# Broadcast rows fetched by DMA, gate columns joined to the key/value strip, and the next group's first products moved ahead of routing, in a one-core decoder layer

## The chip, the cores and the metric

The kernel runs on one core of a Trainium2 chip. The metric is the device time of one execution in microseconds; lower is better. A core has a matrix engine (PE), a vector engine (DVE), a scalar engine (ACT), a general one (POOL, which here issues the gathers and scatters), and SP, which issues the plain transfers in the order in which they stand in its queue. Each engine works through its own instructions in one fixed order and waits for others by semaphores.

## The reference, cut to what matters

For 1024 tokens of 1024 channels:

```python
h = rmsnorm(x, norm1_gain)
(aq, ak, av, mq, mk, mv, mi, mf, mo, gate_a, gate_m) = split_columns(h @ w_in)
att = sliding_window_attention(rope(norm(aq)), rope(norm(ak)), av, sinks)   # 16 query heads, 2 key heads, window 128
i_pre, f_pre = 15 * tanh((mi + i_bias) / 15), 15 * tanh((mf + f_bias) / 15) # 8 + 8 gate columns
hm = mlstm_chunkwise(mq, mk, mv, i_pre, f_pre)                              # 8 heads, a state carried over the tokens
hm = rmsnorm(hm, per head) * sigmoid(mo)
mixed = sigmoid(gate_a) * (att @ w_branch_attn) + sigmoid(gate_m) * (hm @ w_branch_mlstm)
x = x + mixed @ w_out
# experts: 8 heads, each the 16 best of 128 x 128 pairs of sub-keys
q = rmsnorm(x, norm2_gain) @ w_query
s = q . sub_keys;  idx, gate = softmax of the 16 best sums of two scores
x = x + sum over the chosen of gate * gelu(xb . down[idx]) * up[idx]
```

## The kernel before

The 1024 tokens are 8 blocks of 128, taken in 4 groups of two (`GROUPS`). The program has a front, four passes of `front(blocks, fill, hT, following)`, and then `dense()`, in which PE runs all 16,384 experts for blocks 1 to 5. Blocks 0, 6 and 7 (`SPARSE`) get their experts by gathers instead.

One pass of `front` does, in the order of the code: products for the attention's queries (AQ) and for its keys and values (KV); the small products of 16 gate columns with `wif` (L367 to L370); norm and rope of queries and keys; the gates chain, which ends in 8-row tiles `rr` and `wi`; attention (`scores`, `attend`, L429 to L493); mLSTM queries and keys (MQ, MK, into the tile `mqk`); mLSTM values (MV); the decay tile `WT`, made by spreading each row of `rr` over 128 partitions with a product against the identity (L509), adding a triangle with another (L510), and an exponential on ACT; the products of keys and queries (L519); the products that spread `wi` (L528); output gate (MO); the mLSTM output and state, here called the h-stage (L538 to L598); the mixing gates GA, WA, GM, WB (L601 to L620); `normed(following)`, the first norm of the next group; the output products WO (L628); the second norm (L633); and routing, that is the transposes into `xbT`, the router queries WQ (L644) and their scores (L657), which go to memory.

A product with weights takes them as strips `w` of 512 KB through four buffers, in the order of SP's queue. For most products a strip is split in two: ACT casts a high part `whi` (L231), DVE subtracts it for a low part `wlo` (L232), and three matrix products are added (L248 to L250). WA, WB, WO and WQ are not split (L246). The 50 split strips of a group are AQ 8, KV 2, MQ 4, MK 4, MV 8, MO 8, GA and GM 16. The text calls the low part of split strip number n w*n*, counted from 1 over all groups: w101 is the first strip of AQ in the third group, w119 the first of MV there.

`later(blocks)` emits the top-16 selection `topk` of a routed group behind everything of lesser priority (`LATER`): DVE does it in the gaps of the next group. From it come the indices `idx` of block 0, the cells of blocks 1 and 2 (L735), and for blocks 3 to 5 the small products of `spread` (L740 to L767), which `fill` puts one by one beside the products of GA to WQ. POOL gathers 128 rows for block 0 (L773), each consumed on DVE (L787) from three buffers, paced by the products of the front; and it scatters the gates of blocks 1 and 2, 128 instructions each (L804), between the gathers as `BESIDE` says: those of block 1 from gather 24 to 62 on. A scatter that begins a head waits for the 16 of the head before.

A scheduler places the instructions of each engine in one order from priorities and dependences, so a changed program changes that order. PSUM holds three product tiles (`pj`).

Of the kernel before, what the change touches and what calls it, by code (L numbers as in the profile page):

```python
# [12 lines left out]
F32 = mybir.dt.float32  # L13
# [48 lines left out]
def layout(inputs):  # L62
# [3 lines left out]
            np.asarray(inputs["w_out"])[0], np.asarray(inputs["peer_w_query"])[0],  # L66
            w[:, 1024:1280]]
# [4 lines left out]
    a["wif"] = w[:, 3328:3344].reshape(NC, P, 16).transpose(1, 0, 2)  # L72
# [24 lines left out]
def build(nc, tc, a, out, dbg=None):  # L97
# [32 lines left out]
    raw0 = t4([P, 2, P], "raw0")  # L130
    SY.dma_start(raw0[:, 0], a["ident"])
    SY.dma_start(raw0[:, 1], a["tri"])
    identr = cp.tile([P, P], F32R, name="identr")
    trir = st.tile([P, P], F32R, name="trir")
    A.copy(identr, raw0[:, 0])
    A.copy(trir, raw0[:, 1])
# [8 lines left out]
    wifr = t4([P, NC, 16], "wifr")  # L145
    SY.dma_start(wifr, a["wif"])
    wif = [st.tile([P, NC, 16], F32R, name=n) for n in ("wifh", "wifl")]
    A.copy(wif[0], wifr)
    V.tensor_tensor(wif[1], wifr, wif[0].bitcast(F32), ALU.subtract)
    ifb = bcast("ifb", 16, st)  # L150
    band = const("band", [P, 256], pool=st)
    nsinks = bcast("sinks", 16, st)
# [52 lines left out]
    flat = {b: t.rearrange("n i e t -> (n i e t)") for b, t in cells.items()}  # L205
    none = st.tile([P, P * P // ZP], F32, name="none")
# [14 lines left out]
    def wpart(i, q, split):  # L221
        t = wp.tile([P, 4, 256], F32, name="w", bufs=WB)
        SY.dma_start(t, a["wmain"][i, :, 4 * q:4 * q + 4, :])
        for z in [next(clear, None)]:
            if z is not None:
                SY.dma_start(z, none)
        if not split:
            return t, None
        hi = wp.tile([P, 4, 256], F32R, name="whi", bufs=3)
        lo = wp.tile([P, 4, 256], F32R, name="wlo", bufs=3)  # L230
# [27 lines left out]
    def token_major(i, act, nb, n=2, before=nothing):  # L258

        pss = [ppj.tile([P, 512], F32, name="pj") for _ in range(nb)]  # L260
        for u in range(n):
            for q in range(2):
                w = wpart(i + u, q, act[1] is not None)
                for b in range(nb):
                    before()
                    accumulate(pss[b][:, 256 * u:256 * u + 256], pick(act, slice(b * P, (b + 1) * P)),
                               pick(w, slice(0, 256), 4 * q), range(4 * q, 4 * q + 4))
        return [ps[:, :256 * n] for ps in pss]
# [52 lines left out]
    def front(blocks, fill, hT, following):  # L321
# [5 lines left out]
        ms = sp.tile([P, nb, 18], F32, name="qkms")  # L327
        for s in range(3):
            nh = 8 if s < 2 else 2
            pss = token_major(2 * (S_AQ + s) if s < 2 else 2 * S_KV, hT, nb, 2 if s < 2 else 1)  # L330
            for i, b in enumerate(blocks):
# [39 lines left out]
        gt = sp.tile([P, nb, 2, 8], F32, name="gt", bufs=1)  # L371
# [4 lines left out]
        V.tensor_tensor(gf, ps[:, 0:16 * nb].rearrange("p (b k) -> p b k", k=16),  # L376
                        ifb[:, None, :].to_broadcast([P, nb, 16]), ALU.add)
# [38 lines left out]
        A.activation(R[64:72, :tn], m, AF.Exp, scale=-1.0)  # L416
        gc = fp.tile([P, TMAX // P, 72], F32, name="gc")
# [78 lines left out]
        mqk = fp.tile([P, 2, 4, TMAX], F32, name="mqk")  # L496
        mqT, mkT = mqk[:, 0], mqk[:, 1]
        for j, ps in enumerate(feature_major(2 * S_MQ, hT, tn, 4)):
            A.copy(mqT[:, j, :tn], ps)
        for j, ps in enumerate(feature_major(2 * S_MK, hT, tn, 4)):  # L500
            A.activation(mkT[:, j, :tn], ps, AF.Copy, scale=0.125)
# [466 lines left out]
```

## Time and profile before

| what | us |
| --- | --- |
| median of 3 runs | 3464.04 (3463.8 to 3468.68) |
| the profiled execution | 3461.28 |
| its span in the profile | 3459.5 |
| PE busy in the span | 3309.9 (96%) |
| front, up to the first dense product at about 1650 | 1650 |
| dense phase | 1809.5 |

The profile is one execution. Busy time is the time in which an engine has an instruction; the granted clock of PE is given as a share of full speed. A wait is put down to what came last. In the front the four passes overlap at their ends, so a stage's stretch is read from the instructions of its lines.

### The profile page before, as it was taken

To read this page: it belongs to the slowest core of one execution; us is meant where nothing else is said; L and a number is where in the kernel's file an instruction comes from. 1 tells how busy PE (TensorE), PEld (TensorE's weight loads), DVE (VectorE), ACT (ScalarE), POOL (GpSimd) and SP (SyncE) were. 2 spreads that over 40 slices of the span, in tenths; PEclk is the share of its full clock that TensorE was granted. 3 is DMA by queue.
4 is the path that set the end of the run, shared out by engine and by line. 5 is a ranking of instruction groups with operands and counts; after the bars stand their busy time and mean duration, and the time that the engine had idled before them with its cause. 6 is when DMAs were issued, how large, how long until landed. Compare 5 with 4: busy or idle time off the path is not lost.

```text
span 3459.5 us, 54381 instructions
## 1 busy us (share of the span) xinstructions
PE 3309.9 (96%) x20061; PEld 2980.2 (86%) x20061; DVE 2655.4 (77%) x6101; ACT 1289.8 (37%) x2535; POOL 1414.7 (41%) x1028
## 2 busy tenths in 40 slices
PE   7999999987999999997899999999999999999999
PEld 7898988877888888886888889999898989999998
DVE  5342489527889498995999888888888889889885
ACT  6652475225654475545331222222222222222221
POOL 0000001578766475600016545454545545445542
PEclk9899999998999998999999999999999999999999
DMA  7554536786679965877549889888888888888984
GB/s 247 181 169 153 179 117 210 227 233 157 168 208 230 255 182 169 209 213 218 190 149 334 312 309 330 299 322 293 313 298 319 295 308 311 294 311 311 324 286 157
DMA packets 385531, 846.77 MB, mean 245 GB/s; under 512 B 163568, under 2 KB 185840, under 8 KB 385264
## 3 DMA queue, kind: packets, MB, share of 16 engines
q1 hardware_dynamic: 237808, 440.44, 38.7%
q0 software_dynamic: 147456, 402.85, 36.1%
q8 instruction: 158, 2.59, 0.3%
q14 instruction: 109, 0.89, 0.1%
HBM read 780.11 MB, written 63.05 MB: 244 GB/s over the span
## 4 chain that ended last, share of the span: by engine, by line
PE 55%; DVE 11%; DMA 5%; issue 3%; POOL 2%; ACT 1%; DVEq 0%; POOLq 0%; SPq 0%; ACTq 0%
PE ph L860 20%; PE po L883 7%; PE po L887 7%; PE po L886 7%; PE pj L246 4%; PE pj L248 2%; PE pj L250 2%; PE pj L249 2%; PE at L763 2%; DVE g L787 1%; DMA w<-wmain 1%; POOL g L773 1%; DMA g<-up,idx 1%; DMA rawu<-up 1%; DVE oi L755 1%
## 5 line engine op out<-in xcount | busy, mean ns | idle before, releaser
L773 POOL DMA_INDIRECT g<-down,idx x384 | 480.6, 1252 | 1118.9 <-DVE sc L674 506.4
L773 POOL DMA_INDIRECT g<-up,idx x384 | 491.1, 1279 | 755.3 <-DVE acc L821 396.6
L787 DVE CUSTOM_DVE_ANT_0 g<-g,xb 128x1024 f32<-128x1024 f32 x384 | 462.0, 1218 | 124.7 <-DMA g<-down,idx 124.5
L821 DVE SCALAR_TENSOR_TENSOR acc<-g,coef,acc 128x1024 f32<-128x1024 f32 x384 | 491.7, 1280 | 42.4 <-DMA g<-up,idx 31.7
L860 PE MATMUL ph<-xbh,hd 128*128 128x320 f32 x2048 | 470.0, 311 | 35.5 <-ACT hd L848 26.0
L883 PE MATMUL po<-hu,ah 128*128 128x512 f32 x1280 | 499.9, 391 | 1.6 <-ACT ah L872 1.5
L887 PE MATMUL po<-hu,al 128*128 128x512 f32 x1280 | 499.0, 390 | 1.8 <-DVE al L873 1.6
L886 PE MATMUL po<-lu,ah 128*128 128x512 f32 x1280 | 499.2, 390 | 0.0
L804 POOL DMA_INDIRECT cells<-dgate,cell x256 | 442.8, 1730 | 115.0 <-issue 76.5
L860 PE MATMUL ph<-xbh,ld 128*128 128x320 f32 x2048 | 469.8, 311 | 3.3 <-DVE ld L849 3.1
L860 PE MATMUL ph<-xbl,hd 128*128 128x320 f32 x2048 | 469.4, 311 | 0.0
L848 ACT CAST hu<-rawu 128x1024 fp32r<-128x1024 f32 x128 | 131.5, 1052 | 754.1 <-PE po L887 556.4
L860 PEld LDWEIGHTS ph<-xbh,hd 128*128 128x128 f32 x2048 | 345.9, 189 | 39.4 <-ACT hd L848 26.4
L232 DVE TENSOR_TENSOR wlo<-w,whi 128x1024 fp32r<-128x1024 f32 x200 | 243.5, 1219 | 167.3 <-ACT whi L231 165.6
L860 PEld LDWEIGHTS ph<-xbh,ld 128*128 128x128 f32 x2048 | 344.6, 189 | 5.1 <-DVE ld L849 5.1
L860 PEld LDWEIGHTS ph<-xbl,hd 128*128 128x128 f32 x2048 | 345.2, 189 | 0.0
L231 ACT CAST whi<-w 128x1024 fp32r<-128x1024 f32 x200 | 209.2, 1047 | 265.6 <-DMA w<-wmain 105.6
L889 DVE TENSOR_TENSOR y<-po,y 128x512 f32<-128x512 f32 x320 | 218.3, 686 | 90.0 <-PE po L887 89.8
L887 PEld LDWEIGHTS po<-hu,al 128*128 128x128 f32 x1280 | 240.7, 188 | 53.8 <-DVE al L873 3.3
L883 PEld LDWEIGHTS po<-hu,ah 128*128 128x128 f32 x1280 | 240.5, 188 | 53.2 <-ACT ah L872 2.4
L886 PEld LDWEIGHTS po<-lu,ah 128*128 128x128 f32 x1280 | 240.7, 188 | 48.6
L249 PE MATMUL pj<-wlo,hT 128*128 128x256 f32 x832 | 246.3, 297 | 8.4 <-DVE wlo L232 8.4
(276 smaller groups left out, 6579.9 us busy)
## 6 DMA issues: line engine op xcount, KB each, us to landing
w<-wmain SPq DMA_DIRECT2D x328, 512.0 KB, 4.8
rawd<-downT SPq DMA_DIRECT2D x128, 512.0 KB, 7.1
rawu<-up SPq DMA_DIRECT2D x128, 512.0 KB, 5.6
gate_d<-stage SPq DMA_DIRECT2D x24, 1024.0 KB, 6.9
g<-gate_d SPq DMA_DIRECT2D x32, 768.0 KB, 12.0
cells<-none SPq DMA_DIRECT2D x128, 128.0 KB, 4.2
ga<-cells SPq DMA_DIRECT2D x64, 256.0 KB, 8.1
x<-x SPq DMA_DIRECT2D x16, 512.0 KB, 6.8
```

Of the source, the lines that this page charges most:

```text
L231: A.copy(hi, t)
L232: V.tensor_tensor(lo, t, hi.bitcast(F32), ALU.subtract)
L249: T.matmul(ps, lh(c), rl(c), start=False, stop=False)
L773: ins = G.indirect_dma_start(out=t, out_offset=None, in_=a[table], in_offset=bass.IndirectOffsetOnAxis(ap=idx[:, s:s + 1], axis=0))
L787: ins = V.tensor_tensor_reduce(out=t, in0=t, in1=xb, scale=1.0, scalar=0.0, op0=ALU.mult, op1=ALU.add, accum_out=act[:, s:s + 1])
L804: ins = G.indirect_dma_start(out=views[s], out_offset=bass.IndirectOffsetOnAxis(ap=cell[:, c:c + 1], axis=0), in_=vals[:, c:c + 1], in_off ...
L821: ins = V.scalar_tensor_tensor(acc, t, g, acc, ALU.mult, ALU.add)
L860: ins = T.matmul(ps[:, u, 0:W], w[:, c, :], x[:, c, u * W:u * W + W], start=first, stop=last)
L883: first = T.matmul(o, ah[:, tok], uh[:, cols], start=(e == 0), stop=False)
L886: T.matmul(o, ah[:, tok], ul[:, cols], start=False, stop=False)
L887: ins = T.matmul(o, al[:, tok], uh[:, cols], start=False, stop=(e == EG - 1))
L889: V.tensor_tensor(y[:, k, cols], o, y[:, k, cols], ALU.add)
```

## The change

Four edits. The gate columns are no longer products of their own: they are 16 more columns of the KV strips (272 wide). `WT` is no longer filled by PE: `rr` is written to memory (`rr_d`, 8 KB) and read back by a transfer that repeats each row over 128 partitions (1 MB); DVE adds the triangle; the exponential is done in place. `wi` goes the same way through `wi_d` into `wib`, and one DVE multiplication of 128 x 1024 takes the place of four. `front` is a generator that yields twice: once after AQ, KV, MQ and MK, once after the second norm's rows. The loop runs the first part of group n+1 there, then the routing of group n, then the rest of group n+1. So MQ and MK no longer stand behind the attention, and `later` of a group starts after the next group's first products. Lastly the tiles move: the sigmoids of the mixing gates no longer have four buffers `gs`, but lie in `gsa`, which shares its place with `mqk`; `sc` shares with `sm`; `oj` has two buffers.

```diff
--- before.py
+++ after.py
@@ layout, build: inputs @@
-            np.asarray(inputs["w_out"])[0], np.asarray(inputs["peer_w_query"])[0],
-            w[:, 1024:1280]]
+            np.asarray(inputs["w_out"])[0], np.asarray(inputs["peer_w_query"])[0]]
...
-    a["wif"] = w[:, 3328:3344].reshape(NC, P, 16).transpose(1, 0, 2)
+    a["wkv"] = np.concatenate([w[:, 1024:1280], w[:, 3328:3344]], axis=1).reshape(NC, P, 272).transpose(1, 0, 2)
...
+    tri = const("tri", [P, P], pool=st)
...
+    rr_d, wi_d = [dp.tile([8, TMAX], F32, name=n) for n in ("rr_d", "wi_d")]
@@ wpart, token_major @@
-        t = wp.tile([P, 4, 256], F32, name="w", bufs=WB)
-        SY.dma_start(t, a["wmain"][i, :, 4 * q:4 * q + 4, :])
+        n = 272 if i == 2 * S_KV else 256
+        t = wp.tile([P, 4, n], F32, name="w", bufs=WB)
+        SY.dma_start(t, a["wkv"][:, 4 * q:4 * q + 4, :] if n > 256 else a["wmain"][i, :, 4 * q:4 * q + 4, :])
...
@@ front @@
+        gt = sp.tile([P, nb, 2, 8], F32, name="gt", bufs=1)
...
+                    V.tensor_tensor(gt[:, i].rearrange("p k h -> p (k h)"), ps[:, 256:272], ifb, ALU.add)
+        mqk = fp.tile([P, 2, 4, TMAX], F32, name="mqk")
+        mqT, mkT = mqk[:, 0], mqk[:, 1]
+        for j, ps in enumerate(feature_major(2 * S_MQ, hT, tn, 4)):
+            A.copy(mqT[:, j, :tn], ps)
+        for j, ps in enumerate(feature_major(2 * S_MK, hT, tn, 4)):
+            A.activation(mkT[:, j, :tn], ps, AF.Copy, scale=0.125)
+        yield
+
...
-        ps = ppj.tile([P, 512], F32, name="pj")
-        for i in range(nb):
-            accumulate(ps[:, 16 * i:16 * i + 16], pick(hT, slice(i * P, (i + 1) * P)), pick(wif, slice(0, 16)),
-                       range(NC))
...
+        WT = fp.tile([P, 8, TMAX], F32, name="WT", tag="mixT")
+        SY.dma_start(rr_d, rr)
+        SY.dma_start(WT, rr_d[None].to_broadcast([P, 8, tn]))
+        wib = fp.tile([P, 4, TMAX], F32, name="wib")
+        SY.dma_start(wi_d, wi)
+        for e in range(2):
+            SY.dma_start(wib[64 * e:64 * e + 64], wi_d[None, e::2].to_broadcast([64, 4, tn]))
+        V.tensor_tensor(WT.rearrange("p h (b t) -> p (h b) t", t=P), WT.rearrange("p h (b t) -> p (h b) t", t=P),
+                        tri[:, None, :].to_broadcast([P, 8 * nb, P]), ALU.add)
...
-        WT = fp.tile([P, 8, TMAX], F32, name="WT", tag="mixT")
         for h in range(8):
-            ps = ppj.tile([P, 512], F32, name="pj")
-            T.matmul(ps[:, :tn], ident[0:8, h:h + 1].to_broadcast([8, P]), rr, start=True, stop=False)
-            T.matmul(ps[:, :tn], identr, trir[:, None, :].to_broadcast([P, nb, P]), start=False, stop=True)
             for i in range(nb):
-                A.activation(WT[:, h, i * P:(i + 1) * P], ps[:, i * P:(i + 1) * P], AF.Exp, bias=gc[:, i, h:h + 1])
+                w = WT[:, h, i * P:(i + 1) * P]
+                A.activation(w, w, AF.Exp, bias=gc[:, i, h:h + 1])
...
-        for j in range(4):
-            ps = ppj.tile([P, 512], F32, name="pj")
-            for e in range(2):
-                T.matmul(ps[64 * e:64 * e + 64, :tn], ident[0:8, 2 * j + e:2 * j + e + 1].to_broadcast([8, 64]), wi,
-                         start=True, stop=True)
-            V.tensor_tensor(qsT[:, j, :tn], ps[:, :tn], mqT[:, j, :tn], ALU.mult)
-            V.tensor_copy(dec[:, j, 0:nb], ps[:, P - 1:tn:P])
+        V.tensor_copy(dec, wib[:, :, P - 1::P])
+        V.tensor_tensor(qsT, mqT, wib, ALU.mult)
...
-        def gates(i):
-            gs = []
-            for ps in feature_major(i, hT, tn, 4, fill):
-                g = fp.tile([P, TMAX], F32, name="gs", bufs=4)[:, :tn]
-                A.activation(g, ps, AF.Sigmoid)
-                gs.append(g)
-            return gs
+        gsa = fp.tile([P, 2, 4, TMAX], F32, name="gsa", tag="mqk")
+
+        def gates(i, s):
+            for k, ps in enumerate(feature_major(i, hT, tn, 4, fill)):
+                A.activation(gsa[:, s, k, :tn], ps, AF.Sigmoid)
+            return [gsa[:, s, k, :tn] for k in range(4)]
...
+        xbs = norm_rows(xs)
+        for x2, b in zip(xs, blocks):
+            SY.dma_start(x2_d[b], x2)
+        yield nextT
+
         xbT = fp.tile([P, NC, TMAX], F32, name="xbT", tag="mixT")
-        xbs = norm_rows(xs)
...
-                sc = t4([P, 8, P], "sc")
+                sc = fp.tile([P, 8, P], F32, name="sc", tag="sm", bufs=2)
...
-                    oj = ks.tile([P, 2, P], F32, name="oj", bufs=3)
+                    oj = ks.tile([P, 2, P], F32, name="oj", bufs=2)
@@ the loop over the groups @@
-        hT = front(g, fill, hT, GROUPS[n + 1] if n + 1 < len(GROUPS) else None)
-        for _ in spreads:
-            pass
+        part = front(g, fill, hT, GROUPS[n + 1] if n + 1 < len(GROUPS) else None)
+        next(part)
+        if behind:
+            for _ in behind[0]:
+                pass
+            for _ in chain.from_iterable(behind[1]):
+                pass
+            queue.append(chain.from_iterable(later(GROUPS[n - 1])))
+        hT = next(part)
+        behind = part, queue
```

The first place is on PE, between the output products of group 0 (`pj<-w,mixT`) and the next work. Before, the second norm's transposes (`tp<-identr,scr x16`) and the router queries (`pj<-xbT,w`) come next, and then the scores and the first split products of group 1:

```order
L246 MATMUL pj<-w,mixT 128x256 x57
L286 MATMUL tp<-identr,scr 128x128 x16
L246 MATMUL pj<-xbT,w 128x256 x64
L657 MATMUL at<-w,qpT 128x128 x20
L248 MATMUL pj<-whi,hT 128x256
L249 MATMUL pj<-wlo,hT 128x256
L250 MATMUL pj<-whi,hTlow 128x256
```

In the change, the split products of group 1 follow at once, 432 instructions up to the end of MK:

```order
L281 MATMUL tp<-identr,scr 128x128 x8
L240 MATMUL pj<-w,mixT 128x256 x57
L242 MATMUL pj<-whi,hT 128x256
L243 MATMUL pj<-wlo,hT 128x256
L244 MATMUL pj<-whi,hTlow 128x256
```

The norm's transposes and the routing stand behind them, and between the scores come the transposes of the new queries:

```order
L243 MATMUL pj<-hTlow,whi 128x256
L244 MATMUL pj<-hT,wlo 128x256
L281 MATMUL tp<-identr,scr 128x128 x16
L240 MATMUL pj<-xbT,w 128x256 x64
L652 MATMUL at<-w,qpT 128x128 x20
L281 MATMUL tp<-identr,qk 128x128 x4
L652 MATMUL at<-w,qpT 128x128 x8
L281 MATMUL tp<-identr,qk 128x128 x4
```

The AQ, KV, MQ and MK products of the next group moved ahead of the routing.

The second place is on PE behind the MO products of group 1, where the h-stage (`vaug`, `C,mqk`, `kw`, `sg`) meets the mixing gates (`pj<-hT,whi` is GA, `pj<-attT,w` is WA). Before:

```order
L248 MATMUL pj<-hT,whi 128x256
L249 MATMUL pj<-hTlow,whi 128x256
L589 MATMUL at<-vaug,kw 64x129 x4
L250 MATMUL pj<-hT,wlo 128x256
L246 MATMUL pj<-attT,w 128x256 x3
L560 MATMUL at<-vaug,WT 128x129
L562 MATMUL at<-C,mqk 128x129
L560 MATMUL at<-vaug,WT 128x129
L562 MATMUL at<-C,mqk 128x129
L246 MATMUL pj<-attT,w 128x256 x4
L286 MATMUL tp<-identr,sg 128x128
L544 MATMUL tp<-identr,mqk 128x128 x4
```

In the change, after 72 of the 96 GA products of this half:

```order
L242 MATMUL pj<-hT,whi 128x256
L243 MATMUL pj<-hTlow,whi 128x256
L244 MATMUL pj<-hT,wlo 128x256
L281 MATMUL tp<-identr,sg 128x128
L553 MATMUL at<-vaug,WT 128x129
L555 MATMUL at<-C,mqk 128x129
L553 MATMUL at<-vaug,WT 128x129
L555 MATMUL at<-C,mqk 128x129
L582 MATMUL at<-vaug,kw 64x129 x4
L281 MATMUL tp<-identr,sg 128x128 x3
L582 MATMUL at<-vaug,kw 64x129 x4
L553 MATMUL at<-vaug,WT 128x129
```

Here the h-stage now runs as one piece of 30 rows without a product between; the last 24 GA products and all of WA stand behind it.

The third place is on DVE, where the gathered rows of block 0 (`g,act<-g,xb`) stand among the low parts of the strips. Before, the last of 13 such rows that all stand between w100 and w101, and what follows:

```order
L787 ISA g,act<-g,xb 128x1024
L787 ISA act 128x1
L787 ISA g,act<-g,xb 128x1024
L787 ISA act 128x1
L232 TENSOR_TENSOR wlo<-w,whi 128x1024 x3
L787 ISA g,act<-g,xb 128x1024
L787 ISA act 128x1
L232 TENSOR_TENSOR wlo<-w,whi 128x1024
L787 ISA g,act<-g,xb 128x1024
L787 ISA act 128x1
L232 TENSOR_TENSOR wlo<-w,whi 128x1024 x2
L787 ISA g,act<-g,xb 128x1024
```

In the change, in the middle of the same group's AQ and KV strips:

```order
L781 ISA g,act<-g,xb 128x1024
L781 ISA act 128x1
L226 TENSOR_TENSOR wlo<-w,whi 128x1024
L331 TENSOR_REDUCE qkms<-sq 128x8
L781 ISA g,act<-g,xb 128x1024
L781 ISA act 128x1
L226 TENSOR_TENSOR wlo<-w,whi 128x1024
L331 TENSOR_REDUCE qkms<-sq 128x8
L226 TENSOR_TENSOR wlo<-w,whi 128x1024
L781 ISA g,act<-g,xb 128x1024
L781 ISA act 128x1
L226 TENSOR_TENSOR wlo<-w,whi 128x1088 x2
```

By count, gathers 24 to 36 stood ahead of w101 before; now 24 to 30 do, and gathers 31 to 40 stand one or two strips apart between w102 and w117, gathers 41 to 47 ahead of w119. The scatters start on POOL after gather 29 instead of 24.

## Rows read from the trace of the kernel before

**Rows 1.** The page: busy time of the engines, and the chain that ended last.
```profile
PE 3309.9 (96%) x20061; PEld 2980.2 (86%) x20061; DVE 2655.4 (77%) x6101; ACT 1289.8 (37%) x2535; POOL 1414.7 (41%) x1028
PE 55%; DVE 11%; DMA 5%; issue 3%; POOL 2%; ACT 1%; DVEq 0%; POOLq 0%; SPq 0%; ACTq 0%
```

**Rows 2.** Stretches up to and from 1650 us: length, busy time by engine, clock, DMA.
```profile
0.00:1650.00 1650.00, 1522.83 (x10077) 1351.25 (x10077) 1104.99 (x3836) 844.57 (x1988) 598.02 (x388) 0.93 0.68 197
1650.00:3459.50 1809.50, 1787.04 (x9984) 1628.92 (x9984) 1550.43 (x2267) 445.25 (x548) 816.68 (x640) 0.99 0.81 289
```

**Rows 3.** What PE waited for: us in total, times, longest.
```profile
PE tp L286 <- ACT scr L308: 48.3, 5, 22.1
...
PE tp L286 <- DVE qk L357: 13.1, 2, 11.3
...
PE at L657 <- ACT sc L660: 5.5, 4, 2.1
```

**Rows 4.** Instruction groups by form on PE, 0 to 1660 us.
```profile
L509 PE MATMUL pj<-rows,identr 8*128 8x256 f32 x64 | 30.8, 571 | 0.0
...
L519 PE MATMUL at<-mqk 64*128 64x128 f32 x128 | 20.4, 429 | 0.0
L250 PE MATMUL pj<-wifh,hTlow 128*128 128x16 f32 x64 | 18.6, 290 | 0.0
...
L528 PE MATMUL pj<-rows,identr 8*64 8x256 f32 x64 | 15.8, 642 | 0.0
```

**Rows 5.** Stretches inside groups: length, PE, PEld, DVE, ACT, POOL, clock, DMA share, GB/s.
```profile
55.00:62.00 7.00, 7.00 (x57) 7.00 (x56) 0.95 (x5) 4.74 (x9) 0.00 (x0) 0.86 0.88 294
62.00:139.00 77.00, 76.14 (x618) 67.62 (x617) 43.40 (x150) 61.11 (x172) 0.00 (x0) 0.97 0.80 248
139.00:160.00 21.00, 21.00 (x77) 12.17 (x77) 5.27 (x11) 6.32 (x18) 0.00 (x0) 0.57 0.15 54
186.00:226.00 40.00, 39.69 (x268) 34.41 (x267) 20.92 (x81) 30.68 (x80) 0.00 (x0) 1.00 0.30 95
...
948.00:997.00 49.00, 47.26 (x276) 38.34 (x274) 41.81 (x193) 29.93 (x79) 27.51 (x18) 0.93 0.62 166
...
1231.00:1318.00 87.00, 84.29 (x697) 73.93 (x697) 84.09 (x337) 68.39 (x186) 58.89 (x36) 0.96 0.60 157
1318.00:1338.00 20.00, 20.00 (x81) 12.06 (x79) 11.74 (x37) 6.53 (x20) 4.96 (x3) 0.62 0.36 109
```

**Rows 6.** Timeline of PE within the MO products of group 2.
```profile
944.10 0.28 PE L250 MATMUL pj<-whi,hTlow 128*128 128x256 f32 x1
944.22 0.28 PE L248 MATMUL pj<-whi,hT 128*128 128x256 f32 x1
```

**Rows 7.** The instructions of L562, 925 to 1000 us: median ns, first and last start.
```profile
L562 PE MATMUL at<-C,mqk x32: 272/374/501, 948.5 to 988.6; 64*128 64x129 f32 x32
```

**Rows 8.** The page: two DMA issues, the weight strips' remainder on DVE.
```profile
L232 DVE TENSOR_TENSOR wlo<-w,whi 128x1024 fp32r<-128x1024 f32 x200 | 243.5, 1219 | 167.3 <-ACT whi L231 165.6
...
gate_d<-stage SPq DMA_DIRECT2D x24, 1024.0 KB, 6.9
...
cells<-none SPq DMA_DIRECT2D x128, 128.0 KB, 4.2
```

**Rows 9.** What DVE waited for, 640 to 840 us.
```profile
DVE g L787 <- DMA g<-down,idx: 86.8, 17, 10.0
```

**Rows 10.** The scatters on POOL from the first on, to the 128th and 78th.
```profile
645.40:977.00 331.60, 215.62 (x128) 0.90 0.71 185
...
645.40:838.00 192.60, 127.39 (x78) 0.88 0.76 200
```

**Rows 11.** Stretches around the scatters and of group 3, columns as in rows 5.
```profile
645.00:751.00 106.00, 89.44 (x472) 78.98 (x472) 32.79 (x68) 24.15 (x58) 82.84 (x58) 0.94 0.79 203
...
751.00:833.00 82.00, 59.80 (x412) 57.41 (x409) 45.06 (x104) 31.10 (x52) 66.03 (x42) 0.80 0.72 192
...
1195.00:1418.00 223.00, 216.55 (x1547) 189.90 (x1545) 192.61 (x696) 132.28 (x325) 141.06 (x83) 0.90 0.66 186
```

More of the change, by code (lines that the diff above doesn't have):

```diff
@@ L128, in bcast @@
         return const(name, [P, n], a[name].to_broadcast([P, n]), pool=pool)
-    raw0 = t4([P, 2, P], "raw0")
-    SY.dma_start(raw0[:, 0], a["ident"])
-    SY.dma_start(raw0[:, 1], a["tri"])
+    raw0 = t4([P, P], "raw0")
+    SY.dma_start(raw0, a["ident"])
     identr = cp.tile([P, P], F32R, name="identr")
-    trir = st.tile([P, P], F32R, name="trir")
-    A.copy(identr, raw0[:, 0])
-    A.copy(trir, raw0[:, 1])
+    A.copy(identr, raw0)
     ident = identr.bitcast(F32)
@@ L144, in build @@
     qkg = bcast("qkg", 128, st)
[L145 to L149, printed above, removed]
     ifb = bcast("ifb", 16, st)
     band = const("band", [P, 256], pool=st)
+    tri = const("tri", [P, P], pool=st)
     nsinks = bcast("sinks", 16, st)
@@ L228, in wpart @@
             return t, None
-        hi = wp.tile([P, 4, 256], F32R, name="whi", bufs=3)
-        lo = wp.tile([P, 4, 256], F32R, name="wlo", bufs=3)
+        hi = wp.tile([P, 4, n], F32R, name="whi", bufs=3)
+        lo = wp.tile([P, 4, n], F32R, name="wlo", bufs=3)
         A.copy(hi, t)
@@ L260, in token_major @@
         pss = [ppj.tile([P, 512], F32, name="pj") for _ in range(nb)]
+        width = 272 if i == 2 * S_KV else 256
         for u in range(n):
@@ L265, in token_major @@
                     before()
-                    accumulate(pss[b][:, 256 * u:256 * u + 256], pick(act, slice(b * P, (b + 1) * P)),
-                               pick(w, slice(0, 256), 4 * q), range(4 * q, 4 * q + 4))
-        return [ps[:, :256 * n] for ps in pss]
+                    accumulate(pss[b][:, 256 * u:256 * u + width], pick(act, slice(b * P, (b + 1) * P)),
+                               pick(w, slice(0, width), 4 * q), range(4 * q, 4 * q + 4))
+        return [ps[:, :256 * (n - 1) + width] for ps in pss]
     def feature_major(i, act, tn, n, before=nothing):
@@ L365, in front @@
         probe("qT", qT, b0)
-        ps = ppj.tile([P, 512], F32, name="pj")
-        for i in range(nb):
-            accumulate(ps[:, 16 * i:16 * i + 16], pick(hT, slice(i * P, (i + 1) * P)), pick(wif, slice(0, 16)),
-                       range(NC))
-        gt = sp.tile([P, nb, 2, 8], F32, name="gt", bufs=1)
         g1 = sp.tile([P, nb, 8], F32, name="g1", tag="g1", bufs=1)
@@ L375, in front @@
         gf = gt.rearrange("p b k h -> p b (k h)")
-        V.tensor_tensor(gf, ps[:, 0:16 * nb].rearrange("p (b k) -> p b k", k=16),
-                        ifb[:, None, :].to_broadcast([P, nb, 16]), ALU.add)
         A.activation(gf, gf, AF.Tanh, scale=1.0 / 15.0)
@@ L494, in front @@
         probe("attT", attT, b0)
[L496 to L501, printed above, removed]
         for s in range(2):
@@ L601, in front @@
         mixT = fp.tile([P, 8, TMAX], F32, name="mixT")
-        def gates(i):
-            gs = []
-            for ps in feature_major(i, hT, tn, 4, fill):
-                g = fp.tile([P, TMAX], F32, name="gs", bufs=4)[:, :tn]
-                A.activation(g, ps, AF.Sigmoid)
-                gs.append(g)
-            return gs
+        gsa = fp.tile([P, 2, 4, TMAX], F32, name="gsa", tag="mqk")
[3 more added lines that the diff above has]
+            return [gsa[:, s, k, :tn] for k in range(4)]
         for s in range(2):
-            gs = gates(2 * (S_GA + s))
+            gs = gates(2 * (S_GA + s), s)
             for k, ps in enumerate(feature_major(2 * (S_WA + s), (attT, None), tn, 4, fill)):
@@ L615, in front @@
         for s in range(2):
-            gs = gates(2 * (S_GM + s))
+            gs = gates(2 * (S_GM + s), s)
             for k, ps in enumerate(feature_major(2 * (S_WB + s), (hmT, None), tn, 4, fill)):
@@ L620, in front @@
                 V.tensor_tensor(mx_, mx_, gs[k], ALU.add)
-        hT = normed(following) if following else None
+        nextT = normed(following) if following else None
         xs = []
@@ L636, in front @@
             transposed(xbT[:, :, i * P:(i + 1) * P], xb, gains[:, 2])
-            SY.dma_start(x2_d[b], x2)
             if b in SPARSE:
@@ L661, in front @@
                 SY.dma_start(sc_d[b, q], sc)
-        return hT
     def topk(b):
@@ L921, in build, with fill @@
     hT = normed(GROUPS[0])
+    behind = None
     for n, g in enumerate(GROUPS):
-        spreads = chain.from_iterable(later(GROUPS[n - 1])) if n else iter(())
+        queue = []
         due = [0.0]
-        def fill():
+        def fill(queue=queue, due=due):
             due[0] += QUADS
             while due[0] >= 1.0:
-                next(spreads, None)
+                for q in queue:
+                    next(q, None)
                 due[0] -= 1.0
-        hT = front(g, fill, hT, GROUPS[n + 1] if n + 1 < len(GROUPS) else None)
-        for _ in spreads:
-            pass
+        part = front(g, fill, hT, GROUPS[n + 1] if n + 1 < len(GROUPS) else None)
[8 more added lines that the diff above has]
+        behind = part, queue
+    for _ in behind[0]:
+        pass
+    for _ in chain.from_iterable(behind[1]):
+        pass
     later(GROUPS[-1])
```

## The prediction

> **What bounds the kernel now.** I read the page's busy times first: PE works in 96% of the span and holds over half of the chain that ended last [rows 1]. Cutting the span where the dense phase begins shows two regimes. From 1650 us on PE is busy for 1787 of 1809.5 us; nothing of the change touches that phase, so it stays. In the front PE is busy for 1523 of 1650 us and idle for 127 [rows 2]. So nearly all that can be won lies in PE's own work in the front and in those 127 us. The list of PE's waits says what they are: 48.3 us for the normed rows `scr` before transposes (22.1 of it at the very start, which stays), 13.1 for the roped `qk`, 5.5 for the router scores' evacuation [rows 3]. DVE is the second engine: in the front it works 1105 us, and in the stretch of group 3 from 1195 us it is busy 192.6 of 223 us [rows 2, 11]. There is one stretch in which neither bounds. From 645 to 833 us PE is busy only 149 of 188 us [rows 11], DVE waits 86.8 us for gathered rows in 17 pieces [rows 9], and POOL is in the middle of 128 scatters that last 331.6 us [rows 10]. There the chain of scatter, gather, DVE, low part of a strip, product sets the pace.
>
> **Removed: the gate columns.** Their 192 small products stand in four stretches of 7 us, of which the first is shown [rows 5]; each takes 0.29 us, though only 16 wide [rows 4]. In the strip they are 16 more columns on 48 products per group; at 0.12 us per 256 columns [rows 6] that is 0.4 us. Sum over four groups: -26 us.
>
> **Removed: the row products.** Between attention and MO stand four stretches of 21, 24, 19 and 20 us (first and last shown, [rows 5]), in which PE is busy throughout at a granted clock of 0.57 and 0.62 in those shown. What stays of them is L519, 20.4 us in all [rows 4]. That is 84 - 20.4 = 64 us less, 16 in a group. The busy time of the removed kinds agrees: 30.8 and 15.8 us for L509 and L528, and L510 beside them [rows 4].
>
> **Added: the round trip.** No transfer of this kind is in the trace. A transfer of 128 KB lands after 4.2 us, one of 1 MB after 6.9 [rows 8]; writing 8 KB and reading 1 MB back is at most their sum, 11.1 us, and at least 6.9. It starts while the attention has most of its 77 to 87 us before it [rows 5], and `WT` is needed only behind it; so PE doesn't wait. DVE adds the triangle in its fixed order about 5 us of work after the issue, so it may stand for about 5 us per group; it also pays 2.4 us for that addition (twice the 1.22 us of a 128 x 1024 subtraction [rows 8]) and saves as much in the multiplications by `wi`. Bounds: 0 and 20 us over four groups; I take 0 for PE in the first group, where DVE has slack (43.4 of 77 us, [rows 5]), and count the rest under DVE below. The Trainium skill (DMA: Bandwidth & Descriptors, "Anatomy of one DMA") gives about 2.0 us plus bytes over 436,000 per microsecond for a transfer on the gpsimd path: 2.0 + 4.4 = 6.4 us as an estimate for both legs here, against 11.1 by the rows. By the page the stall on DVE would all but vanish; the sum would be some 5 us lower.
>
> **Moved: MQ and MK.** They are 192 products at 0.12 us [rows 6], 23 us, that now lie before the attention instead of beneath it. What is left needs 53 us of PE (76.1 - 23), and ACT keeps 50 of its 61.1 us in group 0; a chain of eight dependent units does not pack perfectly, so I take 59: 23 + 59 against 77, +5 us per group, +20 in all; bounds 0 and +30 (ACT's and DVE's share of 68 and 84 us in group 3 stays whole). In return they cover PE's waits: three of the four norm gaps (three quarters of 48.3 - 22.1, -20 us) and rope's 13.1 us (-11, the longest).
>
> **Moved: the sigmoids' place.** `gsa` lies where `mqk` lay, so the first sigmoid waits for the last reader of `mqk`, L562 of the group's second block. In group 2 that starts 40.6 us after MO ended at 948 [rows 7]. ACT runs in order: the sigmoid that waits holds the cast of the next strip behind it, which is why only 72 of 96 GA products stand ahead of the h-stage. They last 9 us; then PE has 30 small rows and nothing beside them. Before, WA was done 49 us after MO's end in groups 2 and 3 and 40 in group 0 [rows 5]. Now 24 GA products (3 us) and 32 of WA (some 13) follow the last reader: 40.6 + 16 = 57 against 49. I take +10 in each of the last two groups and +6 and +5 in the first two, where topk crowds DVE less: +31 us; bounds 0 and +50. The Trainium skill (Perfetto Trace Analysis, "Optimization Strategy") says that the same gap repeating on the engine that should be saturated can mean too few buffers for the next tile. This trace has no such gap here, since `gs` has four; by that rule the change makes one.
>
> **PE alone** would give -26 - 64 + 20 - 31 + 31 = -70 us.
>
> **What the gathers take back.** The topk of block 0 and 1 is emitted after 18 more strips' low parts (18 x 1.22 = 22 us [rows 8]) and the triangle's 2.4: about 25 us of DVE work now stand ahead of block 1's cells. PE reaches the end of MO(1) about 36 us sooner (two groups' gate columns and rows, one norm gap, less +5 twice and +6). DVE has to do both the strips and the selection there, so between the two I take the first scatter 12 us later than 645.4, at 657; bounds 620 and 670. From there POOL's own pace counts: 78 scatters with their gathers took 192.6 us, 2.47 us each [rows 10]. By the order, 54 scatters stand ahead of gather 40, 133 us, less 6 for five gathers that went before: 784 us, and 5 to land. The low part behind it is the last but one of MK, so the next group's first products end near 795. Then routing, about 43 us, and attention from about 840, in which gather 47 (78 scatters, 657 + 187 = 844) lets MV's strips through near 850. Attention 59, L519 5 and MO 23 us (192 x 0.12) from 848 lead to 935; with DVE's topk in between I take 938, where before it was 948 [rows 5]: -10 us. Of the 36 us won up to then, and of group 2's own terms, all but 10 goes into the wait for gathers. Behind it: gate columns -6.6, rows -16, attention +5, norm gap -6.5, sigmoids +20: -4. **Sum: -14 us**, 3461.3 - 14 = 3447 for the profiled execution, which lay 2.8 below the median; so **3450** in the median's terms.
>
> **Rivals.**
> PE's saving stays. For it: the norm gaps and row products are real PE time. Against it: the 86.8 us of waits lie just where the first products now go. If the first scatter starts by 620, gather 40 lands by 752 and does not hold MK; then -70 holds: 3394.
> Slower. The mechanism is the gathers between the low parts of AQ to MK: all of routing, topk, quads and spread of the group now stand behind products that wait for POOL. It decides when block 1's cells are ready later than 680: each microsecond then goes straight into MK(2), routing and MV(2). At 695, 38 later than assumed, the sum is -14 + 38 = +24: 3488. For it: DVE is full in group 3's attention, 84 of 87 us, and over its whole stretch [rows 5, 11]; a topk that starts a stage later ends a stage later.
> The change moves waits only: the saving in rows is eaten by DVE's stand at the triangle (20 us), nothing else differs from the sum: 3464 - 14 + 20 = 3470.
>
> **How the numbers follow.** Chances: the sum as worked out 0.45 (its own range 3430 to 3468), PE's saving stays 0.2, slower by the gathers 0.25, moved waits 0.1. The range goes from the second case to the third: 3390 to 3490. A difference of 0.2% (7 us) is what a measurement here can tell. Faster by more: 0.2 of the second, 0.33 of the first, 0.02 of the last: 0.55. Within: 0.09 of the first and 0.08 of the others: 0.17. Slower: 0.25 and the first's last 0.03: 0.28.
>
> **What would show it.** Right: no wif or L509 products, PE's waits for `scr` near 28 us in all; a new wait of PE or ACT around GA for the h-stage in each group; L781's waits for gathers between the first strips of group 2; the first scatter near 657; MO(2) ending near 938; the first dense product some 14 us earlier, and 1809 us from there. Wrong: if gathers no longer stall DVE in group 2, if GA's second half starts right behind its first, or if the dense phase changes its length.

## The result and the profile after

The change made the kernel slower: 3496.34 us median (3492.74 to 3502.77) against 3463.92, a ratio of 1.0099 with a 95% interval of 1.0084 to 1.0113. The prediction said 3450, with 3390 to 3490 as its range. It was wrong in sign.

The page of the changed kernel, busy times and the chain that ended last, against [rows 1]:

```profile
PE 3246.8 (93%) x19709; PEld 2929.0 (84%) x19709; DVE 2667.3 (76%) x6084; ACT 1298.2 (37%) x2538; POOL 1393.9 (40%) x1028
PE 46%; DVE 7%; DMA 3%; issue 2%; ACT 1%; POOL 0%; DVEq 0%; POOLq 0%; ACTq 0%; SPq 0%
```

PE has 63 us less to do, and the span is 35 us longer: the work was removed, and waits took more than its place. Stretches of the changed kernel (length, busy time of PE, weight loads, DVE, ACT, POOL; clock, DMA share, GB/s), the first two against [rows 2], the others in the order of the program:

```profile
0.00:1696.50 1696.50, 1465.58 (x9726) 1303.29 (x9726) 1120.10 (x3835) 853.17 (x1994) 580.48 (x388) 0.92 0.68 196
1696.50:3494.40 1797.90, 1781.27 (x9984) 1625.72 (x9984) 1547.18 (x2250) 445.01 (x545) 813.44 (x640) 1.00 0.82 290
54.50:78.40 23.90, 23.90 (x202) 23.90 (x201) 18.31 (x34) 16.78 (x28) 0.00 (x0) 1.00 0.93 297
78.40:133.00 54.60, 52.16 (x419) 42.21 (x417) 26.75 (x118) 50.38 (x162) 0.00 (x0) 0.98 0.81 262
133.00:137.50 4.50, 4.32 (x41) 3.80 (x40) 2.77 (x4) 4.28 (x9) 0.00 (x0) 0.92 0.44 151
161.00:285.00 124.00, 118.69 (x742) 107.22 (x741) 41.34 (x113) 49.27 (x102) 0.00 (x0) 0.96 0.42 136
314.00:366.00 52.00, 52.00 (x433) 51.95 (x432) 32.94 (x54) 34.28 (x55) 0.00 (x0) 1.00 0.69 226
499.00:652.00 153.00, 130.48 (x751) 114.24 (x751) 131.42 (x494) 57.41 (x128) 32.49 (x30) 0.89 0.65 218
683.00:800.00 117.00, 67.28 (x438) 64.81 (x437) 40.16 (x59) 32.65 (x50) 92.77 (x59) 0.78 0.61 142
```

The front ends 46 us later (1696.5 against 1650), the dense phase is 12 us shorter. The third to fifth rows are MQ and MK, attention with MV, and L517 (the products of keys and queries, L519 before) of group 0: 83 us in place of 98 (62 to 160, [rows 5]). The sixth and eighth run from the end of MO to the first product of WO in groups 0 and 1; they are read below, with e1. The last row is the heart of the loss. It holds the first products of group 2, the same 432 instructions as 314 to 366, which are those of group 1: there 52 us, here 117.

What PE waited for, against [rows 3]:

```profile
PE tp L281 <- DVE sg L574: 42.7, 12, 7.4
PE pj L243 <- DVE wlo L226: 29.0, 5, 12.9
...
PE tp L281 <- ACT scr L303: 23.6, 2, 20.8
...
PE at L652 <- ACT sc L655: 14.7, 9, 4.3
PE tp L281 <- ACT xbT L287: 12.5, 3, 11.3
PE pj L244 <- DVE wlo L226: 10.1, 5, 6.4
```

The norm's waits are gone as forecast: `scr` fell from 48.3 to 23.6 us. In their place stand the low parts of strips, the h-stage (`sg`) and the router's `xbT`.

On DVE, 640 to 860 us, against 86.8 us in 17 waits in the kernel before [rows 9]:

```profile
DVE g L781 <- DMA g<-down,idx: 119.8, 18, 15.5
```

POOL, the first scatter in the timeline, and the stretch of the first 78 scatters, against [rows 10]:

```profile
656.65 1.60 POOL L798 DMA_INDIRECT cells<-dgate,cell  x1 [4.60 <-DVE hTlow L289]
...
656.60:841.00 184.40, 129.51 (x78) 0.82 0.64 149
```

The scatters begin at 656.65 us, right behind the cells of block 1, which DVE has written by 656.37 (by 628.38 in the kernel before, where the first scatter came 17 us later). Gather 47, which stands behind 78 scatters, is issued at 842.80, and DVE reads it at 848.86. Timelines of ACT and then of DVE show what that does to the routing that now stands behind:

```profile
805.65 0.41 ACT L365 COPY kd<-qk 128x256 f32<-128x256 f32 x1 [12.44 <-DVE qk L362]
...
810.34 2.15 ACT L287 ACTIVATE xbT<-tp,gains 128x128 f32<-128x128 f32 x8
```

```profile
801.94 1.22 DVE L781 CUSTOM_DVE_ANT_0 g<-g,xb 128x1024 f32<-128x1024 f32 x1 [5.84 <-DMA g<-down,idx]
...
848.86 1.23 DVE L781 CUSTOM_DVE_ANT_0 g<-g,xb 128x1024 f32<-128x1024 f32 x1 [6.61 <-DMA g<-down,idx]
850.01 2.35 DVE L226 TENSOR_TENSOR wlo<-w,whi 128x1024 fp32r<-128x1024 f32 x2
```

DVE waits for gathered rows, so the rope of group 2 is late; ACT, in its order, waits 12.44 us for the rope with the key copy `kd`; the router's `xbT` for group 1 stands on ACT behind that copy; PE waits 11.3 us for `xbT`.

### The profile page after: what moved, and what is told of

It reads as the page before. It is cut to its first block, busy times and chain, and to the rows that moved or that the text cites. A ratio compares the mean times of both kernels' runs of the same rounds, so it can differ in the third digit from the quotient of the medians.

```text
span 3494.4 us, 53772 instructions
## 1 busy us (share of the span) xinstructions
PE 3246.8 (93%) x19709; PEld 2929.0 (84%) x19709; DVE 2667.3 (76%) x6084; ACT 1298.2 (37%) x2538; POOL 1393.9 (40%) x1028
## 4 chain that ended last, share of the span: by engine, by line
PE 46%; DVE 7%; DMA 3%; issue 2%; ACT 1%; POOL 0%; DVEq 0%; POOLq 0%; ACTq 0%; SPq 0%
PE ph L854 21%; PE po L877 7%; PE po L881 7%; PE po L880 7%; PE pj L240 1%; PE at L757 1%; DMA g<-up,idx 1%; DMA rawu<-up 1%; DVE ld L843 1%; DVE g L781 1%; DVE acc L815 0%; DVE y L883 0%; DMA gate_d<-stage 0%; POOL g L767 0%; DMA g<-down,idx 0%
## 5 line engine op out<-in xcount | busy, mean ns | idle before, releaser
L767 POOL DMA_INDIRECT g<-down,idx x384 | 466.6, 1215 | 1160.2 <-DVE sg L574 537.2
L226 DVE TENSOR_TENSOR wlo<-w,whi 128x1024 fp32r<-128x1024 f32 (+1 forms) x200 | 243.5, 1224 | 139.9 <-ACT whi L225 137.1
L225 ACT CAST whi<-w 128x1024 fp32r<-128x1024 f32 (+1 forms) x200 | 208.5, 1047 | 261.2 <-DMA w<-wmain 143.3
L243 PE MATMUL pj<-wlo,hT 128*128 128x256 f32 (+1 forms) x832 | 245.9, 296 | 29.0 <-DVE wlo L226 29.0
```

Source lines behind the costliest of these rows:

```text
L243: T.matmul(ps, lh(c), rl(c), start=False, stop=False)
L767: ins = G.indirect_dma_start(out=t, out_offset=None, in_=a[table], in_offset=bass.IndirectOffsetOnAxis(ap=idx[:, s:s + 1], axis=0))
```

## The experiments

Stage ends, read from each run's PE timeline (us, rounded; attention: its first transposes of `sm`). Runs e5, e6 and e12 change a buffer only and are told below. A ratio is to the kernel before as it was measured beside that run, at medians from 3461.5 to 3464.9 us; so a difference of some 3 us between two experiments says nothing.

| | before | change | e1 | e2 | e3 | e4 | e7 | e8 | e9 | e10 | e11 |
|---|---|---|---|---|---|---|---|---|---|---|---|
| MO(1) | 549 | 499 | 496 | 506 | 511 | 500 | 499 | 498 | 551 | 494 | 497 |
| WO(1) | 704 | 683 | 671 | 688 | 689 | 683 | 683 | 667 | 701 | 670 | 668 |
| attention(2) | 846 | 878 | 873 | 838 | 865 | 881 | 791 | 815 | 809 | 782 | 761 |
| MO(2) | 948 | 957 | 952 | 935 | 942 | 958 | 873 | 915 | 912 | 865 | 870 |
| MO(3) | 1364 | 1377 | 1368 | 1351 | 1375 | 1394 | 1349 | 1329 | 1366 | 1326 | 1317 |
| WO(3) | 1569 | 1590 | 1569 | 1549 | 1595 | 1613 | 1567 | 1532 | 1582 | 1544 | 1542 |
| dense begins | 1650 | 1696 | 1685 | 1656 | 1687 | 1706 | 1671 | 1640 | 1664 | 1660 | 1649 |

**e1, the sigmoids apart.**

```diff
-        gsa = fp.tile([P, 2, 4, TMAX], F32, name="gsa", tag="mqk")
...
+            gsa = fp.tile([P, 4, TMAX], F32, name="gsa", tag="sm", bufs=2)
```

> The change, with the sigmoids of the mixing gates in the attention's two sm buffers instead of mqk's place; nothing else differs. Theory A (the shared place exposes the h-stage: from the end of MO to the start of WO the change takes 124, 153, 154 and 173 us where the kernel before took 116, 121, 149 and 160, 58 us more in sum): those four stretches come back to within 15 us of before, and the time falls by 30 to 60 us, to 3436 to 3466. Theory B (the gathers between the low parts of the first strips and the late routing set the time): the h-stage stretches shorten, but the first products of group 2 wait longer, and the time falls by less than 12 us.

3481.12 us, ratio to before 1.0061 (1.0043 to 1.0079), 15 us below the change. Its four stretches from MO to WO:

```profile
162.00:279.00 117.00, 115.45 (x743) 104.74 (x742) 41.47 (x115) 46.56 (x101) 0.00 (x0) 1.00 0.43 144
495.00:640.00 145.00, 126.91 (x756) 112.67 (x756) 125.13 (x466) 56.05 (x127) 31.45 (x30) 0.92 0.68 231
952.00:1099.00 147.00, 127.29 (x752) 111.47 (x752) 124.63 (x482) 57.83 (x130) 92.77 (x62) 0.93 0.67 192
1368.00:1533.00 165.00, 154.55 (x990) 136.91 (x991) 156.62 (x612) 86.20 (x212) 75.01 (x50) 0.98 0.79 211
```

Against the change the place costs 7, 8, 7 and 8 us, 30 in sum, of which 15 reach the end. The run lies between the two theories: A's stretches came back, all but the second, which stays 24 us above the kernel before. There the kernel before reads:

```profile
549.00:670.00 121.00, 119.25 (x761) 107.55 (x760) 94.08 (x325) 52.78 (x119) 37.72 (x28) 1.00 0.70 225
```

DVE did 94 us of work in it before and does 125 to 131 now: PE arrives some 50 us sooner, and the selection for blocks 0 and 1 still has to be done.

**e2, rows and columns only** (the old loop order, MQ and MK behind the attention, the sigmoids as in e1).

```diff
-        next(part)
         if behind:
...
             queue.append(chain.from_iterable(later(GROUPS[n - 1])))
+        next(part)
```

> Only the rows by transfer and the gate columns in the KV strips; the order of the kernel before (routing, then AQ and KV, MQ and MK behind the attention), sigmoids in the sm buffers. Theory A and B both say that the new order is what costs, so this is faster than before: by PE's own terms 26 + 64 = 90 us (3374); if the scatters' pace takes back what is won before group 2, some 45 (3420). A rival, that the round trip itself costs on DVE or in SP's queue: 3455 or more.

3449.97 us, ratio 0.9966 (0.9953 to 0.9978): 12 us, where the forecast had 90. PE's busy time in the front fell by 64 us, from 1522.8 [rows 2] to 1458.4. The front, and the stretch from MO(1) to WO(1):

```profile
0.00:1655.50 1655.50, 1458.36 (x9725) 1302.09 (x9725) 1118.92 (x3834) 846.49 (x1990) 598.09 (x388) 0.94 0.68 200
506.00:657.00 151.00, 132.86 (x774) 116.33 (x773) 121.04 (x419) 55.86 (x127) 41.55 (x35) 0.90 0.64 211
```

MO(1) is 43 us sooner, WO(1) 16, MO(2) 13, WO(3) 20, and the first dense product is 5 us later. Neither of the two numbers in the expectation holds, and the rival, 3455 or more, is 5 us off. It can be only a small part: DVE waited 0.3 us for the round trip in this run; SP's queue stood 24.3 us in four waits for the rows to be written out, but ACT's waits for strips grew by 8 us only, from 105.6 to 113.7 in the front. The saving is real where it is made and is taken back twice: 27 us between MO(1) and the end of WO(1), where DVE has 121 us of work in place of 94, and 25 in the tail.

**e3, routing first** (the change with the loop of e2's diff alone).

> The change with the loop's order undone: routing of group n first, then AQ, KV, MQ and MK of group n+1, then its attention; sigmoids in mqk's place as in the change. Theory B: topk is no longer late, the gathers wait where routing can go on, the last routing holds no spread products: 3496 down to about 3440, though the norm gaps (20 us) come back. Theory A alone: no better than the change, 3490 to 3515.

3500.59 us (1.0122, 1.0103 to 1.0141), no better than the change. MO(2) comes 15 us sooner, and nothing of it reaches the end. The first products of group 2, still with MQ and MK, take 98 us, and DVE waits 107.6 us for gathered rows. This speaks against the order of AQ, KV and routing as the cause.

**e4, routing first in the last group only.**

```diff
-        next(part)
+        if n < len(GROUPS) - 1:
+            next(part)
...
+        if n == len(GROUPS) - 1:
+            next(part)
```

> The change, but for the last transition the routing of group 2 stands ahead of the first products of group 3, as before. Theory C (topk of blocks 4 and 5 comes some 87 us later, so that 266 spread products stand among the last WQ and scores; from the end of WO(3) to the end of routing(3) the change takes 83 us, before took 57): that stretch returns to below 62 us and the time falls by 15 to 30 us, to 3466 to 3481. If the spread products only move to another place where PE is the bound: 3490 to 3505.

3514.59 us (1.0156, 1.0137 to 1.0175), a miss. WO(3) to the first dense product shrank from 107 to 94 us, but MO(3) came 17 us later. The loss lies ahead of the attention of group 3: from the end of WO(2) to its first scores it is 137 us in place of 115; from there to the end of MO(3) it is 96, and 97 in the change.

**e5 and e6, the third oj buffer back**, in the change and in e2.

```diff
-        ms = sp.tile([P, nb, 18], F32, name="qkms")
+        ms = sp.tile([P, nb, 18], F32, name="qkms", bufs=1)
...
-                    oj = ks.tile([P, 2, P], F32, name="oj", bufs=2)
+                    oj = ks.tile([P, 2, P], F32, name="oj", bufs=3)
```

> The change with three oj buffers again instead of two (and one instead of two of the small qkms, for room). In the change DVE waits 26.8 us for an oj buffer within the 90 us of the last block's spread products, which end the front. Theory D (the lost oj buffer stretches the spread and with it the tail): that wait falls below 10 us, the end of WO(3) to the first dense product shrinks from 106 us, the time falls by 10 to 25 us, to 3471 to 3486. Theory C (the spread comes late since topk of blocks 4 and 5 comes late, the buffer only moves the wait: the kernel before waited 17 us for oi in the same stretch): within 5 us of the change, 3491 to 3501.

> The run of rows and columns only, with three oj buffers (and one qkms). There DVE waits 27.2 us for oj in the last spread, and the first dense product comes at 1656 us although MO(3) ended 13 us and WO(3) 20 us before that of the kernel before. Theory D: the tail follows WO(3) again, the first dense product near 1632, the time 3450 down to about 3432. Theory C: within 5 us of 3450.

3493.87 (1.0092, 1.007 to 1.0115) and 3443.77 us (0.9946, 0.9922 to 0.997): 2.5 and 6 us, neither clear of the intervals of the two runs. That is nearer to theory C than to D. DVE in the last spread, groups by line, first of the change, then of e5 (busy, mean ns, idle before and its releaser):

```profile
L749 DVE TENSOR_SCALAR oi<-iota,cols 128x128 f32<-128x128 f32 x126 | 39.7, 342 | 0.0
L752 DVE TENSOR_SCALAR oj<-iota,cols 128x128 f32<-128x128 f32 x95 | 26.1, 283 | 26.8 <-PE at L757 26.8
```

```profile
L749 DVE TENSOR_SCALAR oi<-iota,cols 128x128 f32<-128x128 f32 x122 | 38.9, 339 | 28.9 <-PE at L757 28.9
L752 DVE TENSOR_SCALAR oj<-iota,cols 128x128 f32<-128x128 f32 x92 | 25.6, 278 | 0.0
```

The wait moved from one buffer to the next. The tail shrank by 6 us in e5 and by 1 in e6; so the buffer is not its main cause.

**e7, the change with the scatters later.**

```diff
-BESIDE = {1: (24, 62), 2: (66, 124)}
+BESIDE = {1: (48, 86), 2: (88, 124)}
```

> The change with the scatters of block 1 between gathers 48 and 86 and those of block 2 between 88 and 124, instead of from gather 24 and 66 on. Theory B (scatter-slowed gathers between the low parts): gathers 31 to 47 land without scatters between; the first products of group 2 take less than 75 us instead of 116 (683 to 799), the attention of group 2 starts some 40 us sooner; if nothing else takes it back, 3496 down to about 3460; if the scatters then slow the attention and MO of group 2 as much, near 3490. Against theory B: first products still over 100 us.

3464.13 us, ratio 0.9995 (0.9981 to 1.0008): 32 us below the change, level with before. Its waits on DVE from 640 to 860 us, and the first products of group 2, which end at 736:

```profile
DVE g L781 <- DMA g<-down,idx: 5.8, 2, 5.0
```

```profile
683.00:733.00 50.00, 49.42 (x408) 49.15 (x407) 42.96 (x67) 32.59 (x50) 15.24 (x11) 1.00 0.92 329
```

They take 53 us instead of 117, as theory B said. MO(2) comes 84 us sooner than in the change; 25 of them reach the dense phase, the rest goes back behind MO(2), where the scatters now lie.

**e9, the same in the kernel before** (e7's diff).

> The kernel before, with the scatters at gathers 48 to 86 and 88 to 124, as in the run of the change that this brought from 3496 to 3464. If the early scatters cost only what the change put behind them (theory B as the prediction told it): before loses nothing much by them, within 8 us of 3464. If they cost the kernel before as much: 3430 to 3445, and the change is then no better placed against its own baseline than it was.

3473.74 us, ratio 1.0028 (1.0012 to 1.0044): some 10 us slower, which neither forecast had. The early scatters were in the right place for the old order, and not for the new.

**e8, the sigmoids apart and MQ and MK back** behind the attention; AQ and KV stay ahead of routing.

```diff
-        mqk = fp.tile([P, 2, 4, TMAX], F32, name="mqk")
...
         yield

...
+        mqk = fp.tile([P, 2, 4, TMAX], F32, name="mqk")
```

> The change with the sigmoids in the sm buffers, and MQ and MK again behind the attention; AQ and KV of the next group stay ahead of routing. Between this and the run with gates apart (3481) stands only the place of MQ and MK, between this and rows and columns only (3450) only that of AQ and KV against routing. If the 192 products without cover cost what the prediction says (5 us in each group) and carry eight strips into the scatters' stretch: 3455 to 3465. If the order of AQ, KV and routing alone makes topk late: 3475 or more.

3438.77 us, ratio 0.9937 (0.9916 to 0.9959), better than its forecast. Against e1 the place of MQ and MK alone is worth 42 us, and against e2 the new order of AQ, KV and routing is a gain of some 11, with intervals that just overlap. DVE still waits 89.3 us for gathered rows between 640 and 860 us; but the strips of MQ and MK no longer stand ahead of routing there.

**e10 and e11, the scatters later in e1 and in e8** (e7's diff).

> The change with the sigmoids in the sm buffers and the scatters later; MQ and MK ahead of the attention. If the two costs add: 3496 - 15 - 32 = 3449. If MQ and MK ahead of the attention are bad only for the scatters, this comes near the run with gates apart and MQ and MK back (3439); if the move costs by itself (5 us a group, the prediction's term, or more), it stays above 3450.

> Gates apart, MQ and MK behind the attention, scatters later: the run at 3439 with the scatters moved. Its gathers between 640 and 860 us waited 89 us. If the later scatters help here as in the change: 3410 to 3420. If DVE's selection and spread set the end by now, since what is won before group 3 is given back there: 3433 to 3445.

3450.52 (0.9965, 0.995 to 0.9981) and 3446.76 us (0.9948, 0.9932 to 0.9964). e10 lies where its forecast put it if the cost of the sigmoids' place and that of the scatters add; e11 lies 2 us above the higher of its two. It is the pair that tells: with the scatters later, MQ and MK ahead of the attention cost 4 us, with overlapping intervals, instead of 42. So the place of MQ and MK and the place of the scatters are one cost: eight more strips in the stretch in which gathers wait for scatters. In e11 attention(2) starts 54 us before that of e8 and the dense phase 9 us after: what is won before group 3 is given back there.

**e12, the fastest:** e8 with e5's buffers.

> Gates apart, MQ and MK behind the attention, scatters where they were, and three oj buffers (one qkms): the run at 3439 with the buffer that gave 2.5 us to the change and 6 to rows and columns only. If these add: 3433 to 3437, the fastest of all, and 24 to 30 us below the kernel before. If the buffer's gain needs the old order: 3437 to 3443.

3436.89 us, ratio 0.9931 (0.9917 to 0.9945), 25 us below the kernel before; from e8 the step is within the spread of the runs.

## Why the prediction was wrong

**Removed work: right.** L517's stretch in group 0 is 4.5 us in place of 21, MQ and MK take 23.9 us, attention 54.6 (forecast 16 less, 23 and 59). MO(1) ended 50 us sooner, where 36 were forecast; 4 of the difference are the attention of group 0, the rest was not followed up.

**Round trip: right in DVE's stand, too low in time.** In groups 1 to 3 DVE stood until the transfer was there. Group 1, in SP's and DVE's rows:

```profile
414.70 0.30 SPq L416 DMA_DIRECT2D rr_d<-rows  x1
...
416.23 0.33 SPq L417 DMA_DIRECT2D WT<-rr_d  x1
...
424.63 2.29 DVE L422 TENSOR_TENSOR WT<-WT,tri 128x2048 f32<-128x2048 f32 x1 [5.55 <-DMA WT<-rr_d]
```

From the first issue to the addition that is 9.9 us; in groups 2 and 3 it is 11.1 and 11.5, the last above the 11.1 that were taken for the most. In group 0 it is 9.0 at most, since DVE came to it from other work without a wait. The estimate of 6.4 us by the Trainium skill (DMA: Bandwidth & Descriptors, "Anatomy of one DMA") was too low by 3.5 to 5.1. The second issue came 1.5 to 2.0 us after the first, near the 2.0 us that it gives for a small transfer, so the miss is in the read of 1 MB: 8.4 to 9.5 us from its issue, against 4.4. DVE waited 13.3 us in the three groups, within the bounds of 0 and 20; the sum held no term for that wait, though the prediction meant to count it under DVE.

**The sigmoids' place: right in size, half of it in the end.** 31 us were forecast for the four stretches, 30 came by e1, and 15 reach the end. What PE waited for before `sg`, in the kernel before and in e1, against 42.7 us in twelve waits in the change:

```profile
PE tp L286 <- DVE sg L581: 5.9, 5, 3.7
...
PE tp L281 <- DVE sg L574: 23.6, 9, 7.0
```

The rule of the Trainium skill (Perfetto Trace Analysis, "Optimization Strategy"), that a gap repeating on the engine that should be saturated can mean too few buffers, agrees in part: the waits stand in all four groups of the change, and with the sigmoids apart 19 us of them go; 23.6 us stay, so the place is not their only cause.

**The gathers: right up to 850 us.** The first scatter was forecast at 657 and came at 656.65; MK's end at 795 and came at 799; the low part for MV at 850 and came at 850.01. That the first date fits to a microsecond is luck: it was chosen between 620 and 670, and MO(1), one of its two grounds, came 14 us sooner than assumed. What follows from it is not luck: 78 scatters with their gathers took 2.36 us each, where 2.47 were forecast.

**The step that failed** is what was put behind these dates: "routing, about 43 us, and attention from about 840", MO(2) at 938, and "Behind it: ... -4", which has no term for the tail. Routing and rope were taken to go on while DVE waited for gathers 41 to 47. They could not, by the chain from DVE over `kd` to `xbT` shown above. PE's waits from 795 to 957 us and the first scores of the attention:

```profile
PE tp L281 <- ACT xbT L287: 11.3, 1, 11.3
...
PE at L652 <- ACT sc L655: 5.1, 2, 3.6
...
860.41 1.65 PE L446 MATMUL at<-kT,qT 64*128 64x256 f32 x3
```

The attention began at 860 in place of 840: MK ended 4 us late, PE waited 11.3 us for `xbT` and 5.1 for the evacuation of router scores. MO(2) came at 957: 19 us. From MO(2) to MO(3) 420 us were needed, 402 forecast: 18 more. The tail from WO(3) to the first dense product, left at its 81.4 us, took 106.8: 25 more. From MO(3) to the end of WO(3) it was 2 us under the forecast, and the dense phase, which was not to change its length, was 12 us shorter. 19 + 18 + 25 - 2 - 12 = 48 of the 49 us between 3447 and 3496.

**The tail** is the largest of these terms. It goes with the number of spread products that the order of PE puts behind WO(3). That stretch in the kernel before and in the change, its spread products alone (PE and weight loads; clock, DMA share, GB/s):

```profile
1568.80:1650.20 81.40, 18.06 (x120) 16.29 (x119) 0.86 0.78 230
1589.70:1696.50 106.80, 33.06 (x200) 29.24 (x200) 0.79 0.71 206
```

In all fourteen traces 120 instructions of this kind go with a tail of 81 to 82 us (before, e9), 136 with 93 to 94 (e3, e4), 168 with 101 (e5), 200 with 104 to 108 (the change, e2, e6, e7, e8, e11, e12) and 236 with 116 to 117 (e1, e10): some 0.3 us each. The 80 of the change are missing between MO(3) and WO(3), where it was 2 us under the forecast. No run changed their number alone, and why more of them stand there is not shown.

**The cause, step by step.** The experiments lead from the kernel before to the change in four steps, the last three with one difference of place each: rows and columns with their buffers (e2) -12 us, AQ and KV ahead of routing (e8) -11, MQ and MK ahead of the attention (e1) +42, the sigmoids in `mqk`'s place (the change) +15: +34 by these medians, against the 32 measured. The move of MQ and MK stood in the sum at +20.

The rival "slower" had the right mechanism and the wrong point of decision. It needed cells later than 680 us; they came at 656, and the kernel was slower all the same. That first products in the stretch of the scatters are what costs is shown by e7 (without scatters there they take 53 us, 32 us come back), by e9 (nothing comes back in the old order) and by e10 against e11. The chain over `kd` is read from the trace; no run takes it out alone, and e3, in which MO(2) comes 15 us sooner, shows that time won there need not reach the end.

**What "PE alone" missed.** By e2, 64 us less busy time of PE are worth 12. DVE still has the same selection and spread to do in one order, and it is full behind MO(1). The prediction let only the gathers take anything back.

**Left open.** Why more spread products stand behind WO(3) is not settled: e5 and e6 exclude the buffer as the main cause, and e4 shows that an earlier selection shortens the tail by 13 us but costs 17 before. What the 18 us between MO(2) and MO(3) are is not known either: 8 lie in WO(2) and 15 behind it, and ahead of it were 4 less than forecast. The dense phase lasted 1806 to 1810 us in the kernel before, e3, e4 and e9 and 1795 to 1799 in all the others; the 12 us lie in its first 340 us, where the selection of blocks 6 and 7 also runs, which ends 146 to 147 us into the phase in those four traces and 124 to 127 in the others. No run was made for it.

## What to carry to other kernels

Work that leaves the busiest engine was worth here only what the engine behind it could follow: read that engine's busy share in each stage, and ask what it still has to do when the first arrives sooner. When a block of work is moved, check which paced transfers its instructions will then share an order with. Two places can each be harmless and cost 40 us together, as those of MQ and MK and of the scatters did; so try the move with the pacing shifted as well. Look at what a schedule leaves for the end of a phase: a term that nothing in the change touches on paper can still move. A tile that is given the place of another should come from one whose last reader is far behind.

## What was not expected of the hardware

The waits in the first products of group 2, of up to 12.9 us each, cost twice. PE was busy there for 67.3 us at a mean granted clock of 0.78, between its two levels of 1.2 and 2.4 GHz, for instructions that took 52 us at 1.00 in group 1 and in e7 again ran at 1.00. Of the 65 us lost there, some 50 were idle and 15 slower work.
